# RWKV chunk products on half of TensorE's rows or columns: a new order, and the new state as two 64-column products

## The chip, the cores and the metric

The kernel runs on one core of one Trainium2 chip. The metric is device time in microseconds of one execution, the median of several. The profile is one execution of its own; its times are microseconds (us) from the start of its span.

Engines as the profile names them: PE is TensorE, which multiplies matrices (PEld is its loading of weights), DVE is VectorE, ACT is ScalarE, POOL is GpSimd, SP issues DMAs. Matmul results go to PSUM banks, from which VectorE and ScalarE read them.

## The reference

One hybrid decoder layer on 4096 tokens of width 1024: an RMS norm, one input projection, RWKV-7 time mixing (8 heads of 64) beside dilated window attention (8 heads of 64), gates, an output projection, the residual and a final norm. The change lies in the RWKV part, whose core is this recurrence, per head:

```python
def step(S, inp):
    r_t, w_t, k_t, v_t, kk_t, b_t = inp
    sa = jnp.einsum('bhvk,bhk->bhv', S, -kk_t)
    S = (S * w_t[:, :, None, :] + sa[..., None] * b_t[:, :, None, :]
         + v_t[..., None] * k_t[:, :, None, :])
    y = jnp.einsum('bhvk,bhk->bhv', S, r_t)
    return S, y
```

Here `kk` is the normalised removal key, `b = kk * a` with the learning rate `a`, and `w` the decay. The outputs `y` then get a group norm per head and a bonus term.

## The kernel before, in words

The recurrence is worked in chunks of 64 tokens. A tile is 256 tokens, that is 4 chunks, and there are 16 tiles. The 8 heads are taken as 4 pairs `p`, one head of a pair on partitions 0 to 63, the other on 64 to 127. `rwkv()` (L756) handles a tile `i` in these steps:

- `keys`, `decay`, `keys2`, `norms`, `queries` (L847 to L904) make for each pair the scaled keys `BK` and the scaled removal keys and queries `KR`.
- `gram` (L906) multiplies `BK` with `KR` for every chunk and head: 4 products for head 0 into one PSUM tile `pg`, a mask on VectorE into `G`, then 4 products for head 1 into a second `pg`, and its mask. A product of head 0 reads rows 0 to 63 of the array, one of head 1 rows 64 to 127. The PSUM tag `m`, of two banks, is shared with other small products of this part.
- `keysT` and `valuesT` (L930, L937) make transposes.
- `inverse` (L951) inverts a triangular matrix for each chunk and head, into `Xn`: mostly on VectorE, with DMAs between, and with 32x32 products at its end (L1016, L1022).
- `stage` (L1028) is the chain. Tile `i` has 16 stages `s`: chunk `c = s // 4`, pair `p = s % 4`. Each has three parts and one PSUM tile `zy` of 3 x 128 columns, one bank; there are three such banks. Part 0: `KR` times the state `Sbd[p]` (L1041, the full 128x128 array), plus `G` times `V` for both heads (L1043, 64x64); ScalarE copies the result to `Z`. Part 1: `Xn` times `Z` for both heads (L1052, 64x64); ScalarE puts it into `UV`, beside a copy of `V`. Part 2: `BKT` times `UV` (L1057, 128x128, of which only the two diagonal 64x64 blocks are used), and `G` times `UV` for both heads (L1059, 128 rows by 64 columns); VectorE updates the two diagonal blocks of `Sbd[p]` (L1062) and ScalarE copies the output to `Y` (L1064). Which half of the rows and columns the 64x64 products use depends on the parity of the chunk.
- `finish` (L1066) does the group norm and writes the tile's output.

Stage `s` needs the state of stage `s - 4`, the same pair one chunk earlier.

Around this, `fill()` (L626) does the rest of the input projection as filling work: 36 units per tile of 24 matmuls or so each (L706 for blocks of 128 columns, L687 for the values).

Order: `at(t, fn, ...)` collects the calls with a time `t`; they are emitted in order of `t`. For step `k` of a chain, part 2 of stage `k - 2` comes first, then part 1 of `k - 1`, then part 0 of `k`. The chain and the inverse carry a high priority (`HP`). Then Tile orders each engine's instructions at build time with a timeline that it simulates (`schedule_with_timeline_sim=True`): of the instructions that are ready by that timeline, the one with the highest priority goes first, so the order on an engine isn't the order of the code. It also sets all semaphores. An engine works through its own queue in the order so fixed.

The lines of the chain's order, before:

```python
for s in range(16):
    for part in range(3):
        at(t0 + dt * (s + part) + 0.01 * (2 - part), stage, i, st, s, part, hp=HP[1])
```

Of the kernel before, what the change touches and what calls it, by code (L numbers as in the profile page):

```python
# [12 lines left out]
F32 = mybir.dt.float32  # L13
# [3 lines left out]
ALU = mybir.AluOpType  # L17
# [10 lines left out]
NCK = TA // CH  # L28
# [24 lines left out]
UVE = 1  # L53
PSB = (2, 2, 3, 1)
# [5 lines left out]
PRE = (1, 1.5, 3.5, 4, 4.2, 7, 7.2, 9, 9.2)  # L60
# [5 lines left out]
VCE = 0  # L66
# [122 lines left out]
class Layer:  # L189
# [566 lines left out]
    def rwkv(self, then=None):  # L756
# [149 lines left out]
        def gram(i, st, p, h):  # L906

            BK, KR = st["BK", p], st["KR", p]
            if h == 0:
                st["G", p] = sp.tile([128, 2, NCK, 128], F32, tag="G", name=f"G{i}_{p}", bufs=NG)  # L910
            Gt = st["G", p]
            mask = cst[:, C_MASK:C_MASK + 256].rearrange("p (r n) -> p r n", r=2)
            pg = pp.tile([128, NCK, 128], F32, tag="m", bufs=PSB[1], name=f"pg{i}_{p}_{h}")
            hs = slice(h * 64, h * 64 + 64)
            for c in range(NCK):
                P.matmul(pg[:, c, :], lhsT=BK[hs, c, :], rhs=KR[hs, c, :], start=True, stop=True)  # L916
            V.tensor_mul(Gt[:, h].rearrange("p (g r) n -> p g r n", r=2),
                         pg.rearrange("p (g r) n -> p g r n", r=2),
                         mask[:, None].to_broadcast([128, NCK // 2, 2, 128]))
            if h == 0:  # L920
                return
# [106 lines left out]
        def stage(i, st, s, part):  # L1028

            c, p = s // 4, s % 4  # L1030
            par = c % 2
            hb, kc = (64, 64) if par == 0 else (0, 0)
            hk, rc = 64 - hb, 64 - kc
            bs, ks = slice(hb, hb + 64), slice(hk, hk + 64)
            KR, Gt, BKT, Vt, WC = (st[x, p] for x in ("KR", "G", "BKT", "V", "WC"))
            halves = [slice(0, 64), slice(64, 128)]
            if part == 0:
                if s == 0:
                    st["Y"] = ip.tile([128, NCK // 2, 512], F32, tag="Y", name=f"Y{i}", bufs=2)
                st["bank", s] = bank = pp.tile([128, 3, 128], F32, tag="zy", name=f"zy{i}_{c}_{p}", bufs=PSB[2])  # L1040
                P.matmul(bank[:, 0], lhsT=KR[:, c, :], rhs=Sbd[p], start=True, stop=True)  # L1041
                for h, hc in enumerate(halves):
                    P.matmul(bank[bs, 0, hc], lhsT=Gt[ks, h, c, kc:kc + 64], rhs=Vt[ks, c // 2, hc],  # L1043
                             start=False, stop=True, skip_group_check=True, tile_position=(hk, hb))
# [599 lines left out]
```

## Time and profile before

| What | Value |
|---|---|
| Time, median of 3 runs | 3575.5 us (3571.65 to 3581.03) |
| The profiled execution | 3583.4 us; its span 3581.6 us |
| Mean granted TensorE clock | 0.936 of full speed |
| Chain of the RWKV part (first to last L1041) | 770.0 to 2445.5 us |
| DMA, mean | 137 GB/s |
| Instructions | 74520 |

Busy shares by 40 equal slices of the span (a digit is a tenth; 9 is 90% or more), by engine, then the granted clock. Slices 1 to 8 are the front of the kernel (norm and first part of the input projection), 9 to 27 the RWKV part, the rest the attention and the output projection:

```
PE   5989957768999999999999999978788888977878
PEld 4778846657878878788766766767677777743333
DVE  7766745546776676677766667554465555246666
ACT  6455535334555656566645555532566667843333
POOL 4432312223232333334322223200445555656655
PEclk7999979889999999999999999988799999989989
```

How to read rows of the profile: a row of a group gives line, engine, operation, `out<-in` by the program's names, rows times columns of the array for a matmul, the shape (partitions x elements) and type, how many; then busy us, mean ns of one, and the idle time before them with what ended it. A row of the timeline gives start, duration, engine, line, operation and how many were merged into it; its duration runs to the modelled end of the last one, so it overlaps the next row. A row of the windows gives the stretch, its length, then busy us (and instructions) of PE, PEld, DVE, ACT and POOL, the granted clock, the DMA share and GB/s. A row of the waits gives who waited for whom, us in all, times, and the longest.

### The profile page before, as it was taken

The numbers are of one execution on the slowest core, as the hardware profiler recorded it, in microseconds if no ns is written. First come the engines' busy times: TensorE is split into PE (matmuls) and PEld (weight loads), VectorE is DVE, ScalarE is ACT, GpSimd is POOL, SyncE is SP. The second block draws the span as 40 slices with busy tenths as digits, with TensorE's granted clock in tenths as the row PEclk, the third lists the DMA queues.
The fourth block names the chain that finished last, engine by engine and source line by source line (L and its number), as shares of the span: only waits on it lengthen the run. The fifth ranks groups of instructions, "written<-read, shape, count | busy, mean of one in ns | idle before, by whom it ended". The sixth has DMA issues, their size and how long they took to land. (4 is left out here: it accounts for less than half of the span.)

```text
span 3581.6 us, 74520 instructions
## 1 busy us (share of the span) xinstructions
PE 3161.2 (88%) x27788; PEld 2458.3 (69%) x27788; DVE 2213.0 (62%) x5525; ACT 1881.2 (53%) x4174; POOL 1317.5 (37%) x1357
## 2 busy tenths in 40 slices
PE   5989957768999999999999999978788888977878
PEld 4778846657878878788766766767677777743333
DVE  7766745546776676677766667554465555246666
ACT  6455535334555656566645555532566667843333
POOL 4432312223232333334322223200445555656655
PEclk7999979889999999999999999988799999989989
DMA  6234545645454654545533334365755556467553
GB/s 194 88 133 145 163 132 159 195 135 154 121 139 124 183 138 121 143 122 144 154 108 106 105 102 116 79 165 152 146 97 99 100 109 111 124 187 209 169 196 112
DMA packets 644875, 490.59 MB, mean 137 GB/s; under 512 B 329457, under 2 KB 570865, under 8 KB 639473
## 3 DMA queue, kind: packets, MB, share of 16 engines
q1 hardware_dynamic: 644512, 485.83, 50.8%
q8 instruction: 219, 3.59, 0.4%
q14 instruction: 144, 1.17, 0.1%
HBM read 307.65 MB, written 177.77 MB: 136 GB/s over the span
## 5 line engine op out<-in xcount | busy, mean ns | idle before, releaser
L706 PE MATMUL pj<-xF,wf 128*128 128x256 f16 x5376 | 695.7, 278 | 16.1 <-ACT qhl L717 7.5
L706 PEld LDWEIGHTS <-wf 128*128 128x128 f16 x5376 | 503.3, 99 | 113.9 <-issue 17.3
L1319 POOL TENSOR_TENSOR hl<-pt,hl 128x1024 f16<-128x1024 f32 x192 | 368.3, 1928 | 291.5 <-ACT hl L1317 253.9
L537 PEld LDWEIGHTS <-wF 128*128 128x128 f16 x4032 | 395.0, 99 | 93.1 <-issue 38.0
L1559 PE MATMUL o<-wo,yc 128*128 128x512 f16 x1344 | 320.6, 401 | 78.7 <-DVE uC L1579 54.0
L1253 DVE CUSTOM_DVE_ANT_0 jk<-sm,at 128x256 bf16<-128x256 f32 (+1 forms) x768 | 257.9, 388 | 194.4 <-PE sm L1246 192.5
L1310 ACT ACTIVATE pt<-st,pb,esc 128x512 f32<-128x512 f32 (+1 forms) x344 | 257.4, 776 | 194.1 <-PE st L1307 186.3
L1559 PEld LDWEIGHTS <-yc 128*128 128x128 f16 x1344 | 136.6, 103 | 256.8 <-issue 99.9
L1329 PE MATMUL po<-hl,vt 128*128 128x128 f16 (+1 forms) x3528 | 291.5, 234 | 11.0 <-POOL hl L1319 5.5
L537 PE MATMUL ps<-xb,wF 128*128 128x256 f16 x2304 | 279.1, 275 | 20.1 <-ACT xb L422 9.0
L1329 PEld LDWEIGHTS <-vt 128*128 128x128 f16 x3528 | 251.9, 101 | 28.6 <-issue 11.9
L1062 DVE SCALAR_TENSOR_TENSOR S<-S,WC,zy 64x64 f32<-64x64 f32 x512 | 142.7, 279 | 139.6 <-PE zy L1059 104.2
L537 PE MATMUL ps<-xa,wF 128*128 128x256 f16 x1728 | 216.0, 275 | 13.2 <-DVE u L552 11.2
L1246 PE MATMUL sm<-km,qm 66*128 66x256 f16 (+1 forms) x768 | 133.1, 277 | 79.1 <-DMA vt<-vsc 47.6
L1307 PE MATMUL st<-q,k 66*128 66x256 f16 (+1 forms) x768 | 184.9, 271 | 0.0
L1307 PE MATMUL st<-qhh,kst 128*128 128x256 f16 (+1 forms) x768 | 184.3, 270 | 0.0
L687 PE MATMUL pv<-wf,xF 128*128 128x512 f16 x768 | 183.6, 380 | 0.0
L1317 ACT CAST hl<-pt 128x1024 f16<-128x1024 f32 x192 | 181.1, 951 | 3.5 <-PE po L1329 1.0
L881 POOL TENSOR_TENSOR BK<-kk,sg 128x256 f32<-128x256 f32 x64 | 64.5, 1008 | 211.4 <-DVE sg L857 122.1
L1246 PEld LDWEIGHTS <-qm 66*128 66x128 f16 x768 | 78.0, 123 | 89.9 <-issue 34.1
L1299 PE MATMUL st<-at 128*128 128x512 bf16 (+1 forms) x352 | 136.2, 391 | 1.1 <-ACT pt L1310 1.0
L916 PE MATMUL pg<-KR,BK 64*128 64x128 f32 x1024 | 132.6, 290 | 4.6 <-DVE BK L887 2.5
(287 smaller groups left out, 6886.6 us busy)
## 6 DMA issues: line engine op xcount, KB each, us to landing
xF<-xsc SPq DMA_DIRECT2D x96, 512.0 KB
prs<-o SPq DMA_DIRECT2D x96, 256.0 KB
krv<-prs SPq DMA_DIRECT2D x64, 384.0 KB
wr<-in_w_in_dram SPq DMA_DIRECT2D x33, 512.0 KB
xr<-in_x_dram SPq DMA_DIRECT2D x32, 512.0 KB
xZ<-xsc SPq DMA_DIRECT2D x64, 256.0 KB
gC<-gsc SPq DMA_DIRECT2D x16, 1024.0 KB
xo<-in_x_dram SPq DMA_DIRECT2D x32, 512.0 KB
```

Source lines behind the costliest of these rows:

```text
L537: P.matmul(ps[:, 0:HT], lhsT=w[:, u, q % HK, :], rhs=x[:, v, q % HK, :], start=(start and q == 0), stop=(q == 3 * HK - 1), skip_group_chec ...
L687: P.matmul(ps, lhsT=x[v][:, k, s * 128:(s + 1) * 128], rhs=self.fw["v", 2 * u + k // 4][:, k % 4], start=(q == 0), stop=(q == 23))
L706: P.matmul(ps, lhsT=self.fw[b][:, u, k, :], rhs=x[v][:, k, :], start=(q == 0), stop=(q == 23))
L1062: V.scalar_tensor_tensor(Sbd[p][hc, hc], Sbd[p][hc, hc], WC[hc, c:c + 1], bank[hc, 2, hc], op0=ALU.mult, op1=ALU.add)
L1246: P.matmul(ps[:, n % 2, 256 - w:], lhsT=tok(qm[0:66], d, c, n * 128, 128), rhs=chunks(km[0:66], d, c, lo, w), start=True, stop=True)
L1253: V.tensor_tensor_reduce(jk[:, :w], ps[:, r % 2, 256 - w:], mask[:, i, 256 - w:256], 1.0, -3e38, op0=ALU.add, op1=ALU.max, accum_out=mx[:, ...
L1307: P.matmul(ps[:, at_:at_ + w], lhsT=tok(lh, d, c, n * 128, 128), rhs=chunks(rh, d, c, q0 * 128, w), start=False, stop=not st, skip_group_c ...
L1310: S.activation(pt[:, to:to + at_], ps[:, :at_], AF.Exp, scale=esc[:, p:p + 1], bias=pb[:, 0:1])
L1317: S.copy(hl[:, 0, :n], pt[:, :n])
L1319: (G if nsp[0] % HLG[0] < HLG[1] else V).tensor_sub(hl[:, 1, :n], pt[:, :n], hl[:, 0, :n])
L1329: P.matmul(out, lhsT=v[:, b * VW + v0:b * VW + v0 + 128], rhs=rhs, start=start and v0 + part == 0, stop=True, skip_group_check=True)
L1559: P.matmul(ps, lhsT=x[:, v, q % HK, :], rhs=w[:, u, q % HK, :], start=(start and q == 0), stop=(q == 3 * HK - 1), skip_group_check=True)
```

## The change

Three things. `gram` now makes the products of both heads in one call, chunk by chunk, head 0 and head 1 in turn, into two `pg` tiles, and then the two masks. `stage` is split into three functions: `with_state` (the product with the state), `solve` (`Xn` times `Z` of stage `s - 1`, in turn with `G` times `V` of stage `s`, head by head, and their copies) and `new_state`, where the 128x128 product `BKT` times `UV` becomes two products of 128 rows by 64 columns, one for each diagonal block: first the block of the half that the readout doesn't use and its state update, then the two readout products, then the other block and its update. A step emits `with_state` of `k`, `new_state` of `k - 2`, `solve` of `k`. Two constants (`UVE`, `VCE`) that chose ScalarE for copies are gone, and ScalarE still does them.

```diff
-PRE = (1, 1.5, 3.5, 4, 4.2, 7, 7.2, 9, 9.2)
+PRE = (1, 1.5, 3.5, 4, 4.2, 7, 9, 9.2)
...
-        def gram(i, st, p, h):
+        def gram(i, st, p):
...
-            pg = pp.tile([128, NCK, 128], F32, tag="m", bufs=PSB[1], name=f"pg{i}_{p}_{h}")
-            hs = slice(h * 64, h * 64 + 64)
+            pg = [pp.tile([128, NCK, 128], F32, tag="m", bufs=PSB[1], name=f"pg{i}_{p}_{h}") for h in range(2)]
             for c in range(NCK):
-                P.matmul(pg[:, c, :], lhsT=BK[hs, c, :], rhs=KR[hs, c, :], start=True, stop=True)
-            V.tensor_mul(Gt[:, h].rearrange("p (g r) n -> p g r n", r=2),
-                         pg.rearrange("p (g r) n -> p g r n", r=2),
-                         mask[:, None].to_broadcast([128, NCK // 2, 2, 128]))
-            if h == 0:
-                return
+                for h, hs in enumerate((slice(0, 64), slice(64, 128))):
+                    P.matmul(pg[h][:, c, :], lhsT=BK[hs, c, :], rhs=KR[hs, c, :], start=True, stop=True)
+            for h in range(2):
+                V.tensor_mul(Gt[:, h].rearrange("p (g r) n -> p g r n", r=2),
+                             pg[h].rearrange("p (g r) n -> p g r n", r=2),
+                             mask[:, None].to_broadcast([128, NCK // 2, 2, 128]))
...
-        def stage(i, st, s, part):
+        def at_chunk(st, s):
...
+            c, p = s // 4, s % 4
+            hb, kc = (64, 64) if c % 2 == 0 else (0, 0)
+            return (c, p, slice(hb, hb + 64), slice(64 - hb, 128 - hb), kc) + tuple(
+                st[x, p] for x in ("KR", "G", "BKT", "V", "WC"))
+
+        halves2 = [slice(0, 64), slice(64, 128)]
+
+        def with_state(i, st, s):
+            c, p, bs, ks, kc, KR, Gt, BKT, Vt, WC = at_chunk(st, s)
+            if s == 0:
+                st["Y"] = ip.tile([128, NCK // 2, 512], F32, tag="Y", name=f"Y{i}", bufs=2)
+            st["bank", s] = bank = pp.tile([128, 3, 128], F32, tag="zy", name=f"zy{i}_{c}_{p}", bufs=PSB[2])
+            P.matmul(bank[:, 0], lhsT=KR[:, c, :], rhs=Sbd[p], start=True, stop=True)
+
+        def solve(i, st, s):
+            for h, hc in enumerate(halves2):
+                if s > 0:
+                    c, p, bs, ks, kc, KR, Gt, BKT, Vt, WC = at_chunk(st, s - 1)
+                    if h == 0:
+                        st["UV", s - 1] = UV = sp.tile([128, 128], F32, tag="UV", name=f"UV{i}_{c}_{p}", bufs=UVB)
+                        S.copy(UV[ks], Vt[ks, c // 2])
+                    P.matmul(st["bank", s - 1][bs, 1, hc], lhsT=st["Xn"][bs, p * 4 + h * 2 + c // 2, :],
+                             rhs=st["Z", s - 1][bs, hc], start=False, stop=True, skip_group_check=True,
+                             tile_position=(bs.start, bs.start))
+                    if h == 1:
+                        S.copy(UV[bs], st["bank", s - 1][bs, 1])
+                if s < 16:
+                    c, p, bs, ks, kc, KR, Gt, BKT, Vt, WC = at_chunk(st, s)
+                    P.matmul(st["bank", s][bs, 0, hc], lhsT=Gt[ks, h, c, kc:kc + 64], rhs=Vt[ks, c // 2, hc],
+                             start=False, stop=True, skip_group_check=True, tile_position=(ks.start, bs.start))
+                    if h == 1:
+                        st["Z", s] = Z = sp.tile([128, 128], F32, tag="Z", name=f"Z{i}_{c}_{p}", bufs=3)
+                        S.copy(Z[bs], st["bank", s][bs, 0])
+
+        def new_state(i, st, s):
+            c, p, bs, ks, kc, KR, Gt, BKT, Vt, WC = at_chunk(st, s)
+            rc = 64 - kc
+            bank, UV = st["bank", s], st["UV", s]
+            own = ks.start // 64
+            for h in (1 - own, own):
+                hc = halves2[h]
+                if h == own:
+                    for u, uc in enumerate(halves2):
+                        P.matmul(bank[ks, 0, uc], lhsT=Gt[:, u, c, rc:rc + 64], rhs=UV[:, uc],
+                                 start=False, stop=True, skip_group_check=True, tile_position=(0, ks.start))
+                P.matmul(bank[hc, 2, hc], lhsT=BKT[:, c, hc], rhs=UV[:, hc], start=False, stop=True,
+                         skip_group_check=True, tile_position=(0, hc.start))
+                V.scalar_tensor_tensor(Sbd[p][hc, hc], Sbd[p][hc, hc], WC[hc, c:c + 1], bank[hc, 2, hc],
+                                       op0=ALU.mult, op1=ALU.add)
+            S.copy(st["Y"][ks, c // 2, p * 128:(p + 1) * 128], bank[ks, 0])
...
-            for s in range(16):
-                for part in range(3):
-                    at(t0 + dt * (s + part) + 0.01 * (2 - part), stage, i, st, s, part, hp=HP[1])
+            for s in range(18):
+                if s < 16:
+                    at(t0 + dt * s, with_state, i, st, s, hp=HP[1])
+                if s > 1:
+                    at(t0 + dt * s + 0.01, new_state, i, st, s - 2, hp=HP[1])
+                if s < 17:
+                    at(t0 + dt * s + 0.02, solve, i, st, s, hp=HP[1])
```

More of the change, by code (lines that the diff above doesn't have):

```diff
@@ L52 @@
 MXL = 32
-UVE = 1
 PSB = (2, 2, 3, 1)
@@ L65 @@
 UVB = 3
-VCE = 0
 PRN = 1024
@@ L1026, in inverse @@
             st["Xn"] = Xn
-        def stage(i, st, s, part):
+        def at_chunk(st, s):
             c, p = s // 4, s % 4
[L1031 to L1044, printed above, removed]
-                st["Z", s] = Z = sp.tile([128, 128], F32, tag="Z", name=f"Z{i}_{c}_{p}", bufs=3)
-                S.copy(Z[bs], bank[bs, 0])
-            elif part == 1:
-                bank, Z = st["bank", s], st["Z", s]
-                st["UV", s] = UV = sp.tile([128, 128], F32, tag="UV", name=f"UV{i}_{c}_{p}", bufs=UVB)
-                (S.copy, V.tensor_copy, G.tensor_copy)[VCE](UV[ks], Vt[ks, c // 2])
-                for h, hc in enumerate(halves):
-                    P.matmul(bank[bs, 1, hc], lhsT=st["Xn"][bs, p * 4 + h * 2 + c // 2, :], rhs=Z[bs, hc],
-                             start=False, stop=True, skip_group_check=True, tile_position=(hb, hb))
-                (S.copy if UVE else V.tensor_copy)(UV[bs], bank[bs, 1])
-            else:
-                bank, UV = st["bank", s], st["UV", s]
-                P.matmul(bank[:, 2], lhsT=BKT[:, c, :], rhs=UV, start=False, stop=True, skip_group_check=True)
-                for h, hc in enumerate(halves):
-                    P.matmul(bank[ks, 0, hc], lhsT=Gt[:, h, c, rc:rc + 64], rhs=UV[:, hc],
-                             start=False, stop=True, skip_group_check=True, tile_position=(0, hk))
-                for hc in halves:
-                    V.scalar_tensor_tensor(Sbd[p][hc, hc], Sbd[p][hc, hc], WC[hc, c:c + 1], bank[hc, 2, hc],
-                                           op0=ALU.mult, op1=ALU.add)
-                S.copy(st["Y"][ks, c // 2, p * 128:(p + 1) * 128], bank[ks, 0])
@@ L1111, in rwkv @@
                 b = B + PSP * p
-                for o, fn, args in zip(PRE, (keys, decay, keys2, norms, queries, gram, gram, keysT, valuesT),
-                                       ((),) * 5 + ((0,), (1,)) + ((),) * 2):
-                    at(b + o * PSS, fn, i, st, p, *args)
+                for o, fn in zip(PRE, (keys, decay, keys2, norms, queries, gram, keysT, valuesT)):
+                    at(b + o * PSS, fn, i, st, p)
             gen = inverse(i, st)
```

4 lines of the change are left out of this document (1 added, 3 removed).

## The prediction, made before the result was known

> **What bounds the kernel now.** I read the head of the page first, then the busy time by stage, then the groups of TensorE instructions, then single stretches of the timeline.
>
> ```profile
> PE 3161.2 (88%) x27788; PEld 2458.3 (69%) x27788; DVE 2213.0 (62%) x5525; ACT 1881.2 (53%) x4174; POOL 1317.5 (37%) x1357
> ```
> ```profile
> 800.00:2200.00 1400.00, 1364.67 (x12480) 1079.62 (x12479) 952.53 (x2058) 783.89 (x2279) 442.73 (x549) 0.99 0.48 131
> ```
>
> The change touches only the RWKV part, which runs from about 770 to 2455 us. From 800 to 2200 us TensorE is busy 1364.67 of 1400 us (97.5%), VectorE 68%, ScalarE 56%, at a granted clock of 0.99: here a microsecond that TensorE no longer spends is a microsecond off the span. Over the whole span it is busy 88%, so this is the part where it binds hardest. What TensorE waits for in the first stretch is little:
>
> ```profile
> PE pq L1016 <- DVE Tn L1009: 12.1, 7, 4.2
> PE pb L933 <- DVE G L917: 4.9, 3, 2.3
> ```
>
> The page gives groups like this one, of the state product (two records to a product: 512 for 256 stages):
>
> ```profile
> L1057 PE MATMUL zy<-UV,BKT 128*128 128x128 f32 x512 | 111.9, 301 | 0.6 <-ACT UV L1054 0.6
> ```
>
> Matmuls are pipelined, so such durations overlap; what a group costs is the distance from its start to the start of what follows. I use those distances below.
>
> **Part 1, the Gram products (L916).** For each of 64 (tile, pair) calls, head 0 takes 8 records on rows 0 to 63, then head 1 takes 8 on rows 64 to 127.
>
> ```profile
> 1434.74 1.05 PE L706 MATMUL pj<-xF,wf 128*128 128x256 f16 x8
> 1435.72 1.71 PE L916 MATMUL pg<-KR,BK 64*128 64x128 f32 x16
> 1437.36 0.49 PE L1041 MATMUL zy<-S,KR 128*128 128x128 f32 x2
> ```
> ```profile
> 1484.08 1.16 PE L916 MATMUL pg<-KR,BK 64*128 64x128 f32 x8
> 1485.16 2.03 PE L706 MATMUL pj<-xF,wf 128*128 128x256 f16 x17
> ```
> ```profile
> 910.72 0.71 PE L916 MATMUL pg<-KR,BK 64*128 64x128 f32 x4
> 911.36 0.44 PE L1052 MATMUL zy<-Z,Xn 64*64 64x64 f32 x4
> ```
>
> Sixteen records take 1437.36 - 1435.72 = 1.64 us, eight 1.08, four 0.64. From four to eight a record costs 0.11; from eight to sixteen only 0.07, since the second head starts beside the end of the first: two row halves do work at once. Alternated from the start, both heads should run in the time of one, 1.08 to 1.12. In 27 of the 64 calls the sixteen stand together (the first and last):
>
> ```profile
> 771.51 1.71 PE L916 MATMUL pg<-KR,BK 64*128 64x128 f32 x16
> ```
> ```profile
> 2315.44 1.71 PE L916 MATMUL pg<-KR,BK 64*128 64x128 f32 x16
> ```
>
> These save 0.54 each, 14.6 us. In 25 calls the chain's own products cut them (as at 911.36), two pieces costing about 2.0 in all; alternated, each piece costs like half as many records, 2 x 0.64 = 1.3, so 0.7 each, 17.5 us. In 12 calls the projection's L706 or L687 stands between the two heads (8 records at 1484.08, 17 of L706 behind): the second head was late, because its bank was, and will be so again; I count nothing there. Sum **-32 us**; ends 0 (the new order does not overlap) and -41 (all 64 calls gain).
>
> The two masks now start behind all sixteen instead of one beside the second head; the chain uses a Gram one tile later, so projection work hides that. Uncovered it would be one mask of 0.69 us per call:
>
> ```profile
> L917 DVE TENSOR_TENSOR G<-pg,cst 128x512 f32<-128x512 f32 x114 | 77.0, 688 | 60.5 <-PE pg L916 59.1
> ```
>
> **Part 2, the new state.** Now one 128x128 product (L1057), then two 128x64 ones (L1059).
>
> ```profile
> 1494.29 0.49 PE L1057 MATMUL zy<-UV,BKT 128*128 128x128 f32 x2
> 1494.70 0.45 PE L1059 MATMUL zy<-UV,G 128*64 128x64 f32 x4
> 1495.08 0.49 PE L1057 MATMUL zy<-UV,BKT 128*128 128x128 f32 x2
> ```
> ```profile
> 1784.46 0.39 PE L1057 MATMUL zy<-UV,BKT 128*128 128x128 f32 x2
> 1784.77 0.45 PE L1059 MATMUL zy<-UV,G 128*64 128x64 f32 x4
> 1785.15 0.38 PE L946 MATMUL po<-h_rb,ones 128*128 128x256 f32 x1
> ```
> ```profile
> 1785.96 0.38 PE L1057 MATMUL zy<-UV,BKT 128*128 128x128 f32 x2
> ```
>
> In a run of stages one costs 0.41 + 0.38 = 0.79 us, behind other work 0.31 + 0.38 = 0.69; with 0.74 on average, 256 stages cost 189 us. The same pair of records costs 0.41 between products of another shape and 0.31 beside one of its own: each change of shape costs about 0.1. A stretch of small products pays it at both ends:
>
> ```profile
> 1782.40 0.44 PE L1052 MATMUL zy<-Z,Xn 64*64 64x64 f32 x4
> 1782.77 0.66 PE L933 MATMUL pb<-cst,BK 128*128 128x128 f32 x4
> ```
> ```profile
> 1783.57 0.68 PE L1052 MATMUL zy<-Z,Xn 64*64 64x64 f32 x8
> 1784.18 0.44 PE L1089 MATMUL py<-cst,Y 128*128 128x128 f32 x2
> ```
> ```profile
> 1496.58 1.47 PE L706 MATMUL pj<-xF,wf 128*128 128x256 f16 x12
> 1497.89 0.38 PE L1089 MATMUL py<-cst,Y 128*128 128x128 f32 x2
> ```
>
> Four cost 0.37, eight 0.61: 0.06 per record and 0.13 per stretch. Twelve L706 cost 1.31 us before a product of their own shape, 0.109 each, but the eight at 1434.74 took 0.98 before the Gram, 0.11 more. So a stretch costs 0.13 + 0.10 = 0.23 us and 0.06 per record.
>
> After the change a stage has eight such records (two for each 64-column product): 0.48 us in line. The question is how many stretches. The code updates the other half's state on VectorE between the first product and the other three. All of them use one PSUM bank, and this program orders any two engines on one bank:
>
> ```profile
> L1064 ACT COPY Y<-zy 64x128 f32<-64x128 f32 x211 | 54.5, 259 | 46.4 <-DVE S L1062 43.1
> ```
> ```profile
> 1677.67 1.19 PE L1022 MATMUL pq<-Xn,Tn 32*32 32x32 f32 x32
> ```
> ```profile
> 1680.48 0.58 ACT L1024 COPY Xn<-pq 32x512 f32<-32x512 f32 x1
> ```
> ```profile
> 1681.53 1.19 PE L1022 MATMUL pq<-Xn,Tn 32*32 32x32 f32 x32
> ```
>
> The copy to Y waits 43.1 us in all for VectorE's state update, though both only read the bank; the second half of L1022 stands behind ScalarE's reading of other partitions of its bank. So the three later products will wait for the update, and other work will be put between: a **fence** in the middle of each stage. Stages run in threes, as at 1494.29; a whole run would be two stretches for three stages, but runs are often broken (1784.46 stands alone, two more follow at 1785.96). I take 1.0 stretch per stage: 0.48 + 0.23 = 0.71 against 0.74, so 0.03 x 256 = **-8 us**. Ends: no fence and both column halves at once, 6 x 0.06 + 0.5 x 0.23 (a stretch for every second stage) = 0.475, so -68; two stretches in every stage, 0.48 + 0.46 = 0.94, so +51. No row shows two column halves side by side.
>
> The Trainium skill ("TensorEngine Tiling (Array Packing)", Key Properties) says that different tiles execute in parallel, column halves too; with the fence left as it is, it would change little here, since the first product ends before the others begin.
>
> **The added wait.** TensorE takes its queue in order, so if VectorE is late, the fill behind the three products is late too. VectorE has ops of 2 us in its queue, against 0.28 for the update:
>
> ```profile
> L1062 DVE SCALAR_TENSOR_TENSOR S<-S,WC,zy 64x64 f32<-64x64 f32 x422 | 117.6, 279 | 106.3 <-PE zy L1059 72.8 <-ACT V L943 7.1 <-ACT yo L1091 6.0
> L996 DVE TENSOR_TENSOR pm<-XL,Ain 128x1024 f32<-128x1024 f32 x28 | 57.3, 2045 | 4.9 <-ACT XL L987 4.4
> ```
>
> Nearest rows: L933 waits 4.9 us over 57 calls (0.09 each), L1016 12.1 over 28 (0.43, behind a transpose that a DMA releases), L1057 0.6 over 256 stages (0.002, its group's row). The chain's own product is the nearest in kind, but what it waits for is ScalarE's; I take 0.02 x 256 = **+5 us**, ends 0 and 0.43 x 256 = 110.
>
> **Part 3, solve.** X·Z of stage s-1 is to alternate with G·V of stage s. They can run at once, as the timeline shows where both happened to be ready:
>
> ```profile
> 1835.40 0.27 PE L1052 MATMUL zy<-Z,Xn 64*64 64x64 f32 x1
> 1835.41 0.27 PE L1043 MATMUL zy<-V,G 64*64 64x64 f32 x1
> ```
> ```profile
> 1835.79 0.83 PE L706 MATMUL pj<-xF,wf 128*128 128x256 f16 x6
> ```
>
> Eight records in 0.39 us instead of twice 0.37. But mostly X·Z waits for the copy of Z behind the G·V of its own stage:
>
> ```profile
> 1498.76 0.44 PE L1043 MATMUL zy<-V,G 64*64 64x64 f32 x4
> 1499.13 0.49 PE L1041 MATMUL zy<-S,KR 128*128 128x128 f32 x2
> 1499.55 0.44 PE L1043 MATMUL zy<-V,G 64*64 64x64 f32 x4
> ```
>
> The instructions are ordered at build time by what is ready first, so G·V of the next stage goes ahead, as here, and the alternation written in the code falls apart. Only a few more pairs will meet: **-3 us**, ends 0 and -90 (0.37 for nearly every stage). The product with the state (L1041) moves to the front of its step; same records, no cost. No DMA moves, and the counts on VectorE and ScalarE stay.
>
> **Sum.** -32 - 8 + 5 - 3 = **-38 us**: 3583.4 (the profiled execution, 1.8 over its span) becomes 3545. The median of the runs shown, 3575.5, lies 0.2% lower, so **3537 us** there.
>
> **Rivals.**
>
> *No fence, halves together* (0.20). If the update of one half does not hold back the other half's products, and both halves stream at once, part 2 gives -68: -32 - 68 - 3 = -103, so 3473. For it: row halves demonstrably overlap. Against it: the rows of L1064 and L1022. The Trainium skill ("PSUM — Partial Sum Buffer", PSUM bank collisions raise a hardware error) says that two engines may use one bank at once in different quadrants, which is this case; the 43.1 us of L1064 do not decide, as its partitions overlap the update's, L1022 speaks against it.
>
> *Solve does alternate* (0.07). If stages come out staggered instead of in threes, part 3 brings up to -90 on top: 3447.
>
> *The fence costs more than it frees* (0.16, slower). One mechanism: each stage is cut at the fence. Two stretches per stage, +51; TensorE behind VectorE by L933's 0.09 in each, +23; the Gram calls gaining only where now uncut, -15: +59, so 3634. It decides from about 1.6 stretches per stage, where part 2's loss of 0.12 x 256 eats part 1's gain. For it: VectorE is 68% busy with long ops. Against: TensorE hardly waits for the chain today.
>
> *Nothing to see* (0.11). The ordering undoes the Gram's alternation as well (second bank late in most calls) or a loss in part 2 of 30 us cancels it: within 11 us of 3575.5.
>
> **How the numbers follow.** Forecast 0.46, its own range 3505 to 3563; the rivals as given. About 0.3% (11 us) is what a measurement of this kernel can tell from no change. Faster by more: 0.46 + 0.20 + 0.07 = 0.73; within: 0.11; slower: 0.16. The range 3465 to 3600 takes in the forecast, the first rival and the flat one, and half of the slower one.
>
> **What would show it.** Right on part 1: sixteen records of the Gram line in 1.1 us, its distance sum down by 30 us. Right on the fence: the first 64-column product and the other three in separate stretches, TensorE shown waiting for S of VectorE. Wrong: all eight records of a stage within 0.5 us; rows of X·Z and G·V alternating by the hundred; TensorE below 96% busy from 800 to 2100 us, which would mean that the chain or VectorE has become the bound.

## The result, and the profile after

The changed kernel is slower: 3598.2 us (median of 5 runs, 3595.1 to 3606.5) against 3580.3 (5 runs of the kernel before beside them), a ratio of 1.0055 with a 95% interval of 1.0037 to 1.0074. The prediction said 3537 and faster; the time lies inside its range and the sign is wrong. The profiled run has a span of 3593.3 us, before 3581.6.

I read the same views as before. First the busy time by stage (windows; columns as in the row shown with the prediction), of the changed kernel and, for the second stretch, of the kernel before:

```profile
800.00:2200.00 1400.00, 1375.01 (x12814) 1052.35 (x12812) 912.80 (x1997) 758.79 (x2220) 413.43 (x536) 0.98 0.48 132
2200.00:2400.00 200.00, 169.28 (x1347) 135.99 (x1346) 140.53 (x316) 92.68 (x280) 48.95 (x63) 0.67 0.38 92
```
```profile
2200.00:2400.00 200.00, 176.87 (x1515) 131.64 (x1514) 118.36 (x300) 85.15 (x256) 32.59 (x54) 0.91 0.48 117
```

From 800 to 2200 us TensorE is even busier (98.2% against 97.5%). Then it has less to do: 1347 records against 1515, at a granted clock of 0.67 against 0.91. Something else became later while TensorE's supply ran out earlier. Where, the first and last starts of two lines show: the copy to Y (the end of the chain; L1064, after the change L1078), and the weight loads of the filling line that ends last (L687, after the change L685):

```profile
L1064 ACT COPY Y<-zy x256: 242/261/264, 903.6 to 2453.4; 64x128 f32<-64x128 f32 x128
...
L687 PEld LDWEIGHTS <-xF x768: 95/98/153, 1807.3 to 2304.8; 128*128 128x128 f16 x192
```
```profile
L1078 ACT COPY Y<-zy x256: 241/260/265, 906.2 to 2501.4; 64x128 f32<-64x128 f32 x128
...
L685 PEld LDWEIGHTS <-xF x768: 95/98/153, 1732.5 to 2191.0; 128*128 128x128 f16 x192
```

The chain ends 48 us later, the filling work 114 us earlier. TensorE got through its filling sooner and the chain still became later, so the amount of TensorE's work did not set the chain's end.

One round of three stages in the changed kernel (timeline; some engines' rows left out):

```profile
1418.66 0.33 PE L1074 MATMUL zy<-UV,BKT 128*64 128x64 f32 x2
...
1418.92 1.16 PE L912 MATMUL pg<-KR,BK 64*128 64x128 f32 x16
...
1420.02 0.39 PE L704 MATMUL pj<-xF,wf 128*128 128x256 f16 x2
1420.08 0.29 DVE L1076 SCALAR_TENSOR_TENSOR S<-S,WC,zy 64x64 f32<-64x64 f32 x1
1420.34 0.45 PE L1074 MATMUL zy<-UV,BKT 128*64 128x64 f32 x4
1420.39 1.29 DVE L914 TENSOR_TENSOR G<-pg,cst 128x512 f32<-128x512 f32 x2
...
1420.93 0.45 PE L1072 MATMUL zy<-UV,G 128*64 128x64 f32 x4
1421.21 0.28 PE L1074 MATMUL zy<-UV,BKT 128*64 128x64 f32 x2
...
1421.60 0.65 DVE L1076 SCALAR_TENSOR_TENSOR S<-S,WC,zy 64x64 f32<-64x64 f32 x3
1421.69 2.46 PE L704 MATMUL pj<-xF,wf 128*128 128x256 f16 x21
...
1424.19 0.45 PE L1072 MATMUL zy<-UV,G 128*64 128x64 f32 x4
```

Sixteen Gram records, alternating, take 1420.02 - 1418.92 = 1.10 us; before it was 1.64. The fence is there too: the first 64-column products at 1418.66 and 1420.34, their state updates (L1076) at 1420.08 and 1421.60, behind VectorE's other work, and only then the three later products at 1420.93 and 1424.19. Between stand 21 products of filling. TensorE hardly idles for it:

```profile
PE zy L1072 <- DVE S L1076: 2.4, 3, 1.8
```

The readouts of the other two stages begin at 1424.19, 5.5 us behind the first product of the round; in the kernel before, the new states and readouts of three stages took 3 x 0.79 = 2.4 us together by the rows in the prediction. The wait is hidden from TensorE and not from the chain. From the first to the last X·Z of a tile (worked out from the timeline, mean of 16 tiles) the chain takes 76.2 us, before 63.2.

Last, the start of the gate products that prepare the attention (L339 before, L337 after):

```profile
2348.78 1.44 PE L339 MATMUL pz<-xZ,wzs 128*128 128x256 f16 x6 [15.96 <-DMA xZ<-xsc]
```
```profile
2364.82 0.39 PE L941 MATMUL po<-h_rb,ones 128*128 128x256 f32 x1
...
2368.09 1.48 PE L337 MATMUL pz<-xZ,wzs 128*128 128x256 f16 x12
```

Before, TensorE stood still 16 us for their loads, which were issued from 2335 us, 30 us behind the last filling line. After, they come right behind the last product `po` of the RWKV part, though filling ended 177 us before. The attention then starts at 2520, 20 us later than before.

### The profile page after: what moved, and what is told of

Read it like the earlier page. It is cut to its first block, busy times and chain, and to the rows that moved or that the text cites. A ratio compares the mean times of both kernels' runs of the same rounds, so it can differ in the third digit from the quotient of the medians.

```text
span 3593.3 us, 75157 instructions
## 1 busy us (share of the span) xinstructions
PE 3186.7 (89%) x28300; PEld 2450.7 (68%) x28300; DVE 2210.6 (62%) x5525; ACT 1875.3 (52%) x4174; POOL 1316.6 (37%) x1357
## 5 line engine op out<-in xcount | busy, mean ns | idle before, releaser
L1076 DVE SCALAR_TENSOR_TENSOR S<-S,WC,zy 64x64 f32<-64x64 f32 x512 | 135.0, 278 | 190.2 <-PE zy L1074 181.3
L1334 ACT CAST hl<-pt 128x1024 f16<-128x1024 f32 x192 | 181.1, 951 | 14.2 <-PE po L1346 11.7
L685 PE MATMUL pv<-wf,xF 128*128 128x512 f16 x768 | 183.1, 380 | 0.0
L1074 PE MATMUL zy<-UV,BKT 128*64 128x64 f32 x1024 | 144.5, 242 | 1.4 <-ACT UV L1053 1.4
L1048 ACT COPY UV<-V 64x128 f32<-64x128 f32 x256 | 74.0, 295 | 128.0 <-PE zy L1074 123.7
```

The lines of the kernel that those rows point to most:

```text
L685: P.matmul(ps, lhsT=x[v][:, k, s * 128:(s + 1) * 128], rhs=self.fw["v", 2 * u + k // 4][:, k % 4], start=(q == 0), stop=(q == 23))
L1074: P.matmul(bank[hc, 2, hc], lhsT=BKT[:, c, hc], rhs=UV[:, hc], start=False, stop=True, skip_group_check=True, tile_position=(0, hc.start))
L1076: V.scalar_tensor_tensor(Sbd[p][hc, hc], Sbd[p][hc, hc], WC[hc, c:c + 1], bank[hc, 2, hc], op0=ALU.mult, op1=ALU.add)
L1334: S.copy(hl[:, 0, :n], pt[:, :n])
```

## The experiments

Two theories were put against each other. **A**: TensorE's work bounds the RWKV part (the prediction's view). **B**: a loop bounds it: Gram, inverse and chain of tile `i`, whose first buffer is free only when the chain of tile `i - 2` is in its last chunk; filling is cover. For B speaks, in the kernel before, what the first Gram of tile 2 waits for, beside the last copies to Y of tile 0:

```profile
L916 PE MATMUL pg<-KR,BK x16: 272/272/373, 948.4 to 950.7; 64*128 64x128 f32 x16
its engine sat idle before it (us, times) until:
  DVE KR L900: 1.5, 2
```
```profile
L1064 ACT COPY Y<-zy x2: 261/261/261, 960.4 to 970.1; 64x128 f32<-64x128 f32 x2
```

Tile 2 starts 22 us before tile 0 ends, and so it stays: over tiles 2 to 15 the start lies 4 to 23 us before the end of the chain two tiles earlier. KR and G have eight buffers, four for a tile. A tie between the two tiles shows in the last product that reads pair 0's KR in tile 0, and the first write of pair 0's KR in tile 2, which takes the same buffer:

```profile
943.66 0.39 PE L1041 MATMUL zy<-S,KR 128*128 128x128 f32 x2
```
```profile
945.60 2.37 DVE L885 TENSOR_TENSOR KR<-kk,ei 128x256 f32<-128x256 f32 x1
```

Over tiles 2 to 15 this write starts 0.3 to 3.6 us behind the last record of that product in 11 of 14 tiles (the other three: 6 to 14 us), and in the changed kernel 0.3 to 4.0 us behind it in all 14. The other three pairs come 20 us or more behind theirs in both kernels, so of the four only pair 0 waits for its KR buffer.

All runs (the time, its ratio to the kernel before beside it with the 95% interval; and from the timeline of the profiled run: the chain per tile, the start of the last `po`, of the last L687, of the first gate product, of the last copy to Y, and of the first score product of the attention, L1299 before):

| kernel | us | ratio | chain | po | L687 | gate | Y | att. |
|---|---|---|---|---|---|---|---|---|
| before | 3580.3 | 1 | 63.2 | 2322 | 2305 | 2349 | 2453 | 2499 |
| after | 3598.2 | 1.0055 [1.0037, 1.0074] | 76.2 | 2365 | 2191 | 2368 | 2501 | 2520 |
| e1 no fence | 3579.0 | 0.9974 [0.9961, 0.9988] | 61.8 | 2327 | 2215 | 2331 | 2450 | 2485 |
| e2 Gram only | 3578.7 | 0.9977 [0.9961, 0.9994] | 63.9 | 2334 | 2272 | 2337 | 2465 | 2490 |
| e3 order only | 3585.1 | 0.9997 [0.9983, 1.0012] | 63.0 | 2320 | 2296 | 2345 | 2454 | 2493 |
| e4 fence only | 3630.5 | 1.0119 [1.0097, 1.0140] | 79.3 | 2401 | 2222 | 2404 | 2537 | 2554 |
| e5 less filling | 3607.5 | 1.0077 [1.0051, 1.0102] | 61.7 | 2347 | 1988 | 2351 | 2475 | 2513 |
| e6 short inverse | 3562.2 | 0.9919 [0.9888, 0.9950] | 63.7 | 2277 | 2320 | 2370 | 2370 | 2477 |
| e7 no fence, short inverse | 3499.6 | 0.9765 [0.9749, 0.9781] | 61.3 | 2221 | 2245 | 2282 | 2328 | 2408 |
| e8 nine buffers | 3576.5 | 0.9983 [0.9965, 1.0000] | 61.5 | 2314 | 2238 | 2319 | 2441 | 2483 |
| e9 fence, short inverse | 3547.5 | 0.9907 [0.9881, 0.9933] | 77.9 | 2309 | 2252 | 2311 | 2439 | 2460 |
| e10 halves, Gram, old order | 3563.3 | 0.9959 [0.9946, 0.9973] | 60.9 | 2306 | 2221 | 2310 | 2432 | 2465 |
| e11 products on GpSimd | 3571.4 | 0.9980 [0.9968, 0.9992] | 63.7 | 2333 | 2250 | 2336 | 2452 | 2492 |
| e12 longer chain | 3595.7 | 1.0054 [1.0034, 1.0073] | 74.9 | 2349 | 2225 | 2350 | 2492 | 2510 |
| e13 fence, gates apart | 3577.1 | 0.9994 [0.9980, 1.0008] | 75.4 | 2376 | 2186 | 2222 | 2489 | 2505 |
| e14 e10, gates apart | 3551.2 | 0.9923 [0.9904, 0.9941] | 59.1 | 2322 | 2221 | 2268 | 2423 | 2445 |

### One part at a time

**e1_no_fence**: the changed kernel with both updates behind the last product.

```diff
             for h in (1 - own, own):
                 ...
                 P.matmul(bank[hc, 2, hc], lhsT=BKT[:, c, hc], rhs=UV[:, hc], ...)
-                V.scalar_tensor_tensor(Sbd[p][hc, hc], ...)
+            for hc in halves2:
+                V.scalar_tensor_tensor(Sbd[p][hc, hc], ...)
```

> After, with both state updates behind all products of the stage instead of one between them. Fence theory (the update between the products cuts each stage, so the chain of a tile takes 76 us from its first to its last product X·Z instead of 63): chain back to 58 to 65 us per tile, time 3540 to 3572 us. Rival, order (the product with the state at the front of its step, and solve, lengthen the chain): chain stays at 74 to 78 us, time 3590 to 3605. TensorE view (only its summed time counts): 3545 to 3565, whatever the chain's length.

**e2_gram_only**: the kernel before with the new `gram`.

```diff
-        def gram(i, st, p, h):
+        def gram(i, st, p):
...
+            for c in range(NCK):
+                for h, hs in enumerate((slice(0, 64), slice(64, 128))):
+                    P.matmul(pg[h][:, c, :], lhsT=BK[hs, c, :], rhs=KR[hs, c, :], start=True, stop=True)
```

> Before, with the Gram products of both heads in turn and nothing else. All theories: sixteen records together in 1.09 us instead of 1.64, chain 62 to 65 us per tile. TensorE view: 13 us less in the Gram's distances, so 3564 to 3570 where before is 3580. If the loop chain, Gram, inverse sets the end of the RWKV part, TensorE's saving shows only in part: 3570 to 3582.

**e3_order_only**: the three new functions in their new order, with the old Gram and the 128x128 product.

```diff
         def new_state(i, st, s):
             ...
+            P.matmul(bank[:, 2], lhsT=BKT[:, c, :], rhs=UV, start=False, stop=True, skip_group_check=True)
+            for u, uc in enumerate(halves2):
+                P.matmul(bank[ks, 0, uc], lhsT=Gt[:, u, c, rc:rc + 64], rhs=UV[:, uc], ...)
+            for hc in halves2:
+                V.scalar_tensor_tensor(Sbd[p][hc, hc], ...)
```

> Before, with the new order (product with the state first, new state, then solve with the two products in turn), but the new state with one 128x128 product and its updates behind all products, and the old Gram. Fence theory: chain 61 to 66 us per tile, time 3570 to 3588. Rival, order: chain 74 to 78 us, time 3595 to 3615.

**e4_fence_only**: the kernel before with the two 64-column products and the update between them.

```diff
         def stage(i, st, s, part):
             ...
-                P.matmul(bank[:, 2], lhsT=BKT[:, c, :], rhs=UV, start=False, stop=True, skip_group_check=True)
...
+                for h in (1 - own, own):
+                    hc = halves[h]
+                    if h == own:
+                        for u, uc in enumerate(halves):
+                            P.matmul(bank[ks, 0, uc], lhsT=Gt[:, u, c, rc:rc + 64], rhs=UV[:, uc], ...)
+                    P.matmul(bank[hc, 2, hc], lhsT=BKT[:, c, hc], rhs=UV[:, hc], ...)
+                    V.scalar_tensor_tensor(Sbd[p][hc, hc], ...)
```

> Before, with the new state as two 64-column products and an update between them, as in the change; old order, old Gram. Fence theory: chain 74 to 80 us per tile, time 3598 to 3620, above the changed kernel by the Gram's gain that is missing. Rival, order: chain 61 to 65 us, time 3570 to 3582. TensorE view: 8 us less in its distances, 3572.

In all four runs the chain has the length that the fence theory named. The times of e1 and e4 lie above its bands (3579.0 against 3540 to 3572, 3630.5 against 3598 to 3620), beside a kernel before that took 3587.4 us here and 3580.3 where the bands come from.

The fence is the whole loss: by itself it makes the kernel 1.2% slower (e4), without it the same change is 0.26% faster (e1), the order does nothing that can be measured (e3). The alternating Gram is worth 0.23% (e2). And without the fence column halves do run at once, as the timeline of e1 shows for one stage of eight records:

```profile
1413.52 0.27 PE L1074 MATMUL zy<-UV,BKT 128*64 128x64 f32 x1
1413.53 0.27 PE L1072 MATMUL zy<-UV,G 128*64 128x64 f32 x1
1413.63 0.22 PE L1074 MATMUL zy<-UV,BKT 128*64 128x64 f32 x1
1413.63 0.34 PE L1072 MATMUL zy<-UV,G 128*64 128x64 f32 x3
1413.81 0.28 PE L1074 MATMUL zy<-UV,BKT 128*64 128x64 f32 x2
1414.02 0.28 PE L704 MATMUL pj<-xF,wf 128*128 128x256 f16 x1
```

Two products start 0.01 us apart, and the stage takes 0.50 us. The Trainium skill ("TensorEngine Tiling (Array Packing)", Key Properties) says that different tiles can execute in parallel, and lists 128x64 as two tiles just above; this stage agrees. Over all stages the new state and the readout take 122 us of TensorE, before 193 (sum of the distances from each record to the next start, a distance above 0.6 us counted as 0.6, so that idle time stays out); with the Gram's 14 less, these products free about 84 us. The other products of the chain (X·Z, G·V and the product with the state) take 18 us more, 286 against 268, so e1 frees about 66 us of TensorE's time in all. It gains 9. That is where theory A broke.

### What bounds it

**e5_less_fill**: the filling loop ends after 16 of 24 products.

```diff
-            for q in range(24):
+            for q in range(16):
```

> The kernel before with less filling work: each 128-column block of the filling projection (L706) makes 16 of its 24 products and leaves out the third partial product; the RWKV chain is untouched. One third of 5376 records at 0.109 us is 195 us of TensorE time. Theory A (TensorE's work bounds the RWKV part): the time falls by nearly all of it, to 3390 to 3420. Theory B (the loop of Gram, inverse and chain through buffers for two tiles bounds it, and filling only covers it): the last copy to Y stays within 40 us of 2453, the time falls by 0 to 60 us, and TensorE's busy share from 800 to 2200 us drops to 88% or less.

It is 0.77% slower, although TensorE has some 195 us less to do. Theory A's 3390 to 3420 did not come, and B's gain of 0 to 60 us did not either. The rows are of e5, the last one of the kernel before:

```profile
800.00:2200.00 1400.00, 1286.92 (x10835) 988.95 (x10832) 942.56 (x2052) 770.14 (x2258) 439.27 (x549) 0.91 0.49 135
...
2000.00:2200.00 200.00, 151.10 (x1051) 121.03 (x1051) 125.16 (x269) 89.63 (x267) 55.74 (x71) 0.61 0.31 73
2200.00:2400.00 200.00, 174.58 (x1219) 139.65 (x1218) 117.44 (x277) 82.89 (x245) 42.67 (x51) 0.61 0.27 66
```
```profile
2000.00:2200.00 200.00, 200.00 (x1625) 138.68 (x1624) 134.88 (x298) 105.08 (x313) 54.56 (x93) 1.00 0.38 106
```

Once filling is gone (from 1988 us on) the granted clock is 0.61; in the kernel before it was 1.00 and 0.91 in these two stretches. Busy time there is partly slow time: 174.58 us for 1219 records. From 800 to 2200 us TensorE is still 92% busy (88% or less was expected): the filling that is left is used up sooner. The last copy to Y comes 22 us later than before, and the stretch at 0.61 is not all of it: the chain of tile 10 (counted from 0) had ended 25 us later already (last copy to Y at 1982 against 1957), while there was filling and the clock was 0.91 to 1.00. The Trainium skill ("TensorE: Matmul & The Clock Gate", Part 1) says that a throttled clock is the default state and activity releases it; these rows agree. How much of the loss the clock explains was not isolated.

**e6_short_inverse** and **e7_no_fence_short_inverse**: the same cut in the kernel before and in e1. Its sums take 4 of 16 terms; the rest of the inverse is left out.

```diff
-                rhs = (A[:, 1] if e == 0 else XH).rearrange("p c f -> p f c")
-                n = PRN // 256
+                rhs = (A[:, 1] if e == 0 else XH).rearrange("p c f -> p f c")[:, :, 0:4]
+                n = 8
```

> The kernel before with a shorter inverse on VectorE: the two blocks of sums at L996 and L998 take 4 of their 16 terms, in one product and one reduction each in place of two of twice the size; the other 12 terms are left out. VectorE's stretch falls by about 13 us per tile, TensorE's work is the same. Theory A: no change beyond 10 us. Theory B: a round of two tiles loses about 13 us; over 8 rounds up to 100, but TensorE, which has only about 3% to spare under this part, leaves it 30 to 70 us: 3510 to 3550; the last copy to Y moves ahead by 50 or more.

> The same shorter inverse (4 of 16 terms at the two blocks of sums, the others left out) in the changed kernel with both state updates behind all products (no fence). Theory A: as without the shorter inverse, 3579 +- 10, since TensorE's work is the same. Theory B: the TensorE time that the halves and the Gram free (about 84 us in distances) can be used once the loop is shorter, so it gains more over its own base than the kernel before did from the same cut: 60 to 110 us, 3470 to 3520.

Not one matmul is gone, and the time falls by 29 us (0.9919 of 3582.7, by its interval 18 to 40) and by 84 (0.9765). e6 stays above B's 3510 to 3550, e7 lies in its band. The cut shortens the way from the Gram's last DMA (L926) of a tile to its first X·Z by 13.7 us (68.4 to 54.7). In e6 the chain ends 83 us earlier than before, but filling ends 15 us later, and in 8 of 14 tiles pair 0's KR is now written 13 to 34 us behind the product that frees its buffer. The loop has slack there, and TensorE stands in the way:

```profile
2200.00:2400.00 200.00, 197.76 (x1549) 144.82 (x1548) 88.78 (x248) 82.50 (x252) 29.91 (x48) 0.87 0.43 115
```

Together, e1's freed TensorE time and the shorter loop bring 84 us where each alone brings 9 and 29. There are **two limits**, near each other: the loop, and TensorE's total. Freeing one shows its worth only where the other gives way.

**e9_fence_short_inverse**: e7 with the fence back.

> The changed kernel, with its fence, and the shorter inverse (4 of 16 terms at the two blocks of sums on VectorE, the others left out). Against the same cut without the fence (3499.6) only the place of the two state updates differs. If the fence's price is the length of the chain, which stands in the loop whatever TensorE does: chain 13 to 16 us per tile longer, 40 to 90 us above 3499.6, so 3540 to 3590. If its price were TensorE's time alone (about 70 us of distances, as between the fenced and the unfenced kernel): TensorE has work waiting to the end of this run, and it would be the same 70; then the chain per tile must stay within 5 us of 61.

Some 50 us above e7 (0.9907 against 0.9765) lies in the first band and not far below the 70 of the second, so the time does not tell the theories apart. The chain does: 77.9 us, not 61. But TensorE is nearly full here as well,

```profile
800.00:2200.00 1400.00, 1385.39 (x13157) 1067.06 (x13156) 839.52 (x2032) 793.26 (x2321) 429.48 (x559) 0.99 0.49 134
```

so both prices of the fence may count in this kernel. Against e6, which has the old products and the same cut, e9 is not slower (the intervals overlap) though its chain is 14 us per tile longer. In e6 the first gate product comes 50 us behind the filling and 93 behind the last `po`, so the loop had room there and a longer chain costs little; e9 also has less TensorE work, and the two were not separated.

**e12_longer_chain**: the kernel before with three more copies on ScalarE in each stage; no fence, and TensorE's work as it was.

```diff
-                S.copy(Z[bs], bank[bs, 0])
+                S.copy(Za[bs], bank[bs, 0])
+                S.copy(Zb[bs], Za[bs])
+                S.copy(Z[bs], Zb[bs])
...
-                (S.copy if UVE else V.tensor_copy)(UV[bs], bank[bs, 1])
+                S.copy(UVa[bs], bank[bs, 1])
+                S.copy(UV[bs], UVa[bs])
```

> The kernel before with a longer chain and nothing else: Z goes through two more copies on ScalarE, UV through one more (0.26 us each by the rows of L1046 and L1054, so 0.78 us per stage, up to 12.5 us per tile, at the cost of 200 us of ScalarE time in all). TensorE's instructions are the same, and there is no fence. Loop theory: the chain per tile becomes 6 to 13 us longer; the fence made it 13 longer for 20 us of time, so 3590 to 3610 beside a before of 3582 (ratio 1.003 to 1.007), with the last copy to Y 20 to 50 us later. TensorE theory: no change (ratio within 0.002), since TensorE's work is the same and filling work is there to put between. If ScalarE's load were the cause, its waits would show at work outside the chain.

This is the cleanest of them. The chain grows by 11.7 us per tile, the time by 0.54%; the change made it 13.0 and 0.55%. Filling runs ahead as in the changed kernel (its last L687 at 2225 instead of 2305), TensorE is *busier* with the same work, and the chain ends late. The chain's and the Gram's products do cost TensorE more in distances, cut up as they are (611 against 585 us for the same records), but the filling still ends 80 us earlier, so TensorE's time is not what ran out.

```profile
800.00:2200.00 1400.00, 1382.27 (x12499) 1085.48 (x12497) 941.81 (x2038) 944.89 (x2873) 414.17 (x538) 0.99 0.48 131
2200.00:2400.00 200.00, 170.08 (x1248) 132.80 (x1248) 116.32 (x286) 107.85 (x339) 47.50 (x58) 0.72 0.41 101
```
```profile
L1069 ACT COPY Y<-zy x256: 242/261/264, 896.0 to 2491.6; 64x128 f32<-64x128 f32 x128
```

ScalarE is busy 945 of 1400 us here (784 before), so its load is not quite excluded as a part of it.

### How the end of the loop reaches the time

The columns `po`, `L687` and `gate` of the table go together: the first gate product starts 1 to 5 us behind the last `po`, or 37 to 50 behind the last L687, whichever is later (e13 and e14, made to break this, apart). The kernel before is of the second kind, by 24 us (2349 against 2325). By this, 24 us is the most that freed TensorE time can bring before the loop sets the start; in e1 the start moves by 18 (to 2331) and is of the first kind. The changed kernel is of the first kind.

**e13_fence_gates_apart** and **e14_halves_gates_apart**: the gate and first score products no longer take banks of the tag `m` in turn, in the changed kernel and in e10.

```diff
-            self.banks = self.banks + [(pp, "m", PSB[1])]
```

> The changed kernel, with its fence; the gate products and first score products ahead of the attention (L337, L1263) no longer use banks of the tag m in turn with their own. If it is the shared bank that holds them behind the last po, they begin at about 2235 instead of 2368, soon after the filling work (2191) and their weights (2219). If the changed kernel loses time because the chain ends late (last copy to Y 2501, the attention 18 us behind it), the time stays within 10 us of 3598. If it loses it through the late gates alone, it falls to 3560 to 3580.

> The same in the kernel of e10 (old order, alternating Gram, halves without a fence), whose last copy to Y is at 2432, last gate product at 2455 and attention at 2465. If the shared bank holds the gates, they begin at about 2265 instead of 2310 and end before the chain; the attention then begins at about 2450, and the time falls by 5 to 15 us, to 3548 to 3558. With fewer banks the gates themselves may be slower; if their end stays behind 2450, nothing is gained.

```profile
L337 PE MATMUL pz<-xZ,wzs x768: 269/273/437, 2222.2 to 2447.4; 128*128 128x256 f16 x192
```
```profile
2200.00:2400.00 200.00, 184.19 (x1710) 148.28 (x1707) 145.08 (x383) 100.33 (x294) 50.31 (x61) 0.87 0.56 145
```

In e13 the gates begin 154 us ahead of the last `po` (2222 against 2376): it was the shared bank that held them. The time falls to that of the kernel before (0.9994), though the chain still takes 75.4 us per tile; the clock in the gap rises from 0.67 to 0.87. The time is in the second band. But the same edit also makes the kernel without the fence faster (e14 0.9923, e10 0.9959), so the 0.6% that it brings here is not the fence's price alone. Fence and order together cost 0.96% with the shared bank (after against e10) and 0.71% without it (e13 against e14), and these two prices do not differ beyond their intervals: most of the price remains when the gates are out of the way. The attention then starts 16 us behind the last copy to Y, so the end of the chain takes the place of the gates; both come from the same loop.

### Versions that were to be faster

**e8_no_fence_nine_buffers**: e1 with nine buffers of KR and G, for pair 0 of the next tile.

```diff
-NBUF = (8, 8, 5)
+NBUF = (8, 9, 5)
...
-            KR = sp.tile([128, NCK, 128], F32, tag="KR", name=f"KR{i}_{p}", bufs=NB)
+            KR = sp.tile([128, NCK, 128], F32, tag="KR", name=f"KR{i}_{p}", bufs=NG)
```

> The changed kernel without the fence, with nine instead of eight buffers for KR and G, so that pair 0 of a tile needs not wait for the end of the chain two tiles earlier (room made by one buffer fewer for four small tags and two fewer in the gates' weight loads). Nothing is left out. Theory A: 3579 +- 10. Theory B: the first Gram of a tile starts up to 20 us earlier, a round of two tiles shrinks, 3510 to 3560, and the last copy to Y comes 20 to 70 us earlier; if the other pairs then wait for their buffers just as long, nothing is gained (3579).

**e10_halves_gram_old_order**: the new Gram of e2, and in `stage` the products of e4 with both updates behind them.

```diff
         def stage(i, st, s, part):
             ...
+                for h in (1 - own, own):
+                    ...
+                    P.matmul(bank[hc, 2, hc], lhsT=BKT[:, c, hc], rhs=UV[:, hc], ...)
+                for hc in halves:
+                    V.scalar_tensor_tensor(Sbd[p][hc, hc], ...)
```

> The kernel before, in its old order of the stages, with the alternating Gram and with the new state in two products of 64 columns and both updates behind all products. Candidate for the best version. Loop theory: 3570 to 3580 beside a before of 3582, as without the fence in the new order, since loop and chain are the same. If the new order of the stages was worth something by itself, this one is slower than 3579 by more than 5 us.

**e11_no_fence_products_on_gpsimd**: e1 with half of the inverse's large products on GpSimd.

```diff
-                    V.tensor_mul(pv, XL[:, e, h:h + n, None, :].to_broadcast([128, n, 16, 16]),
-                                 rhs[:, None].to_broadcast([128, n, 16, 16]))
+                    (V, G)[h // n].tensor_mul(prs[-1], XL[:, e, h:h + n, None, :].to_broadcast([128, n, 16, 16]),
+                                              rhs[:, None].to_broadcast([128, n, 16, 16]))
```

> The changed kernel without the fence, with the inverse's two blocks of sums shared out: in each, VectorE makes the product of the first half (1.9 us) while GpSimd makes that of the second half, and then VectorE reduces both (second product buffer in place of two buffers of the tag f and one of the gates' weight loads). Nothing is left out. The product of 1024 elements costs GpSimd 2.4 us by its nearest row (L1489), so 1.5 to 2 us less in each block, 3 to 4 per tile. Loop theory: 13.7 us less per tile gave 79 us, so 3.5 give 10 to 25: 3555 to 3570. TensorE theory: 3579 +- 5. If GpSimd takes over 4 us for it or is late, the inverse is no shorter and the time stays or rises.

e8 gains nothing over e1 that can be told: the first Gram comes up to 41 us ahead of the end of the chain two tiles earlier, but a tile then takes 154 us instead of 146 from there to its first X·Z. e8 stands on e1, where the wait for KR's buffer was loose already (4.6 to 28 us behind the freeing product in 8 of 14 tiles); with nine buffers the write comes 5 to 19 us ahead of that product in every second tile. Nine buffers under the fence were not run. So the buffer is one tie of the loop, and that it alone closes it is not shown. e11 misses as well: GpSimd needs more than the 2.4 us that I took,

```profile
L992 POOL TENSOR_TENSOR pm<-XL,Ain 128x1024 f32<-128x1024 f32 x16 | 62.3, 3896 | 91.2 <-ACT XL L982 56.0 <-DVE XL L981 25.5 <-PE zy L1051 6.1
```

3.9 us for this one and 3.2 for the other. The way from the Gram's last DMA to the first X·Z is 2.9 us shorter than in e1 (65.0 against 67.9) and the chain 1.9 longer, so nothing comes of it. e10 lies below its band (3563.3 against 3570 to 3580) and is as fast as e1 or a little faster (the intervals overlap). With the gates apart (e14) it is the fastest complete kernel, 3551 us, 0.77% below the kernel before.

## Why the prediction was wrong

That the time lies inside the range is no merit: the range reaches to 3600 only to take in half of the slower rival.

**What bounds the kernel: wrong, and this is the step that failed.** "Here a microsecond that TensorE no longer spends is a microsecond off the span" was read off 97.5% busy. But the work that makes it so busy is filling, which goes wherever there is room. e5 takes a part of it away and is slower, e6 touches no matmul and is faster, e12 has the same matmuls and is slower. What set the changed kernel's time was the loop of Gram, inverse and chain: a chain 13.0 us per tile longer went with 20 us of time, and copies on ScalarE that made it 11.7 us longer gave 19. What closes the loop is open in part: the timing speaks for KR's buffer, and no run shows it by itself. The quoted row could not tell a bound from a well-covered wait; a KR that is written 2 us after its buffer comes free, tile after tile, could have hinted at it.

**The new state: right in TensorE's time, wrong in what it left out.** The distances fall from 192.6 to 184.7 us, -8 as forecast, and the fence is where it was put. But the fence was priced by TensorE's stretches and TensorE's waits alone. Its real price is that the state of a stage is ready later: 13 us per tile, which is about 2.4 us for each round of three stages (13 x 3 / 16). That term is missing from the sum.

**The added wait: right as a number, wrong as a price.** TensorE waits 2.4 us for S between 800 and 2160 us (+5 was forecast). The wait of the chain behind the filling work that is put into the gap was not asked for.

**The Gram: right in kind, half in size.** A call that alternates takes 1.10 us, as forecast, but the sum of the distances falls only from 125 to 112 us: -13 instead of -32. The trace has 30 pieces of eight records at 1.11 us, one head alone, as before (36 at 1.08): the order at build time undoes much of the alternation.

**Solve: wrong in sign.** The forecast was -3 us, and nothing for the product with the state. In the changed kernel the distances of X·Z and G·V rise from 177 to 185 us and those of the product with the state from 91 to 99; records of X·Z and G·V stand next to each other 109 times, before 140. By itself the new order has no effect on the time that can be told (e3). So the products that the sum counts freed 5 us of TensorE's time, not 43; by TensorE's time alone the kernel would have been about as fast as before, and it is 20 us slower.

**The rivals.** The slower one has the right sign and a wrong mechanism: it, too, counted only TensorE's time (+59). The rival without a fence describes e1 well in TensorE's time (122 us is -70 against the forecast -68), yet it would have given 3473 where e1 measured 3579. The rival that saw nothing comes nearest in TensorE's time, partly by its own mechanism (the order undoes much of the Gram's alternation), and has no term for the chain either. The one in which solve alternates did not come. Of the signs named for being wrong, "TensorE below 96% busy" did not come: the chain became later with TensorE at 98.2%.

## What to carry to other kernels

An engine that is kept full by work which fits anywhere isn't shown to be the bound by its busy share: test it, by making another path shorter (e6) or longer (e12) with that engine's work unchanged, and price a change by what it adds to a recurrence as well as by the engine's time. A wait put between two steps of a recurrence is paid by the recurrence even where the waiting engine fills the gap. And two limits can lie so close (here 24 us) that relieving one shows little until the other is relieved: e1's changes brought 9 us on their own and about 55 beside the shorter inverse (84 against 29).

## What the runs showed of the hardware

- Two row halves, alternating, run wholly side by side, as forecast: sixteen records in 1.10 us, eight of one half alone in 1.08. Column halves do so too, which no row of the kernel before showed: two products start 0.01 us apart, and eight records take 0.50 us (e1).
- Less work went with a slower clock here: 0.61 with 1051 TensorE records in 200 us (e5), 1.00 with 1625 in the same stretch of the kernel before.
